# A two-layer hybrid decoder on one core: the first layer's feed-forward starts by token tile

## The chip, the core and the metric

The kernel runs on one core of a Trainium2 chip. Its time is device microseconds of one execution. In the texts below PE is TensorE, which multiplies matrices, DVE is VectorE, ACT is ScalarE, POOL is GpSimd, and SP is the queue from which the transfers are issued. PSUM is the memory into which PE writes, in banks of 128 x 512 floats; SBUF holds all other tiles.

## What is computed

256 tokens of width 2048 go through two layers. Each layer has a mixer (sliding-window attention beside an RWKV-7 recurrence) and a feed-forward network of width 5632. Both are framed by a modulation from a condition vector and by a layer norm. Cut to what matters here:

```python
mod = einsum('bd,de->be', silu(c), w_ada[l]) + b_ada[l]      # six vectors of 2048
sh_m, sc_m, gt_m, sh_f, sc_f, gt_f = split(mod)
u = x * (1 + sc_m) + sh_m
mix = concat([attention(u @ w_in[l]), rwkv7(u @ w_in[l])]) @ w_out[l]
x = layer_norm(alpha * x + gt_m * mix, ln1_w[l], ln1_b[l])
u = x * (1 + sc_f) + sh_f
gate, up = split(u @ w_gate_up[l])
x = layer_norm(alpha * x + gt_f * ((silu(gate) * up) @ w_down[l]), ln2_w[l], ln2_b[l])
```

## The kernel before, in words

**Tiles.** The 256 tokens are two token tiles of 128. The width of 2048 is 16 row blocks of 128 (`kts`, `kt`), over which every projection sums. A float32 product is made of three products of a faster format: each operand is split into a high part (its cast to that format) and a low part (what the cast lost), and PE adds high x high, high x low and low x high. For weights ACT makes the high part (line 380) and DVE the low part (line 381). For activations the two parts are the halves of a tile `u`, one for each row block.

**Weights.** `steps` (line 364) loads 512 KB at a time into one of four `raw` tiles and splits it, usually into three `hi` and two `lo` tiles. If it is given a `room`, it splits into tiles from there instead, so that the parts can be kept. `stream` (line 390) issues the products of a list of row blocks. For each token tile in `ts` and each 512 columns it issues lines 402 (high x high), 403 (the weights' low part) and 405 (the activations' low part). It returns the split weights, and a later call that is given them as `held` uses them again.

**The feed-forward's start.** `channel` (line 1115) ends the mixer: the last 512 columns of the output projection are finished for token tile 0 first and then for tile 1, since `SPLIT_O` is (8, 8). Behind each tile come the gate (line 1163), the residual (1164) and the statistics (1165), all on DVE. `normalise` then takes the mean and variance (1064), adds the epsilon (1066), raises to the power -1/2 on POOL (1067), and scales the tile's four pieces, two on DVE (1078) and two on ACT (1076).

`inputs` (line 1080) makes the `u` tiles out of the normalised rows `z`, eight row blocks at a time. It has two ways, chosen by `apart`. With `apart` 0 it calls `make_u`: PE transposes a pair of row blocks for both token tiles (354), ACT makes a float32 copy and the high part, 256 columns each (358, 360), and DVE subtracts (361). With `apart` 8 the first eight row blocks go by token tile:

```python
for t in range(2):
    for k4 in range(0, apart, 4):
        ... # four transposes of tile t (line 1100)
        V.tensor_scalar(uf, pt_[:, i * P:(i + 1) * P], a[:, kt:kt + 1], b[:, kt:kt + 1], ALU.mult, ALU.add)
        S.copy(u[:, 0, :], uf)
        V.tensor_tensor(u[:, 1, :], uf, u[:, 0, :].bitcast(F32), ALU.subtract)
    yield kts[0:apart], (t,)
```

These are lines 1105 (DVE), 1106 (ACT) and 1107 (DVE), with 128 columns each. The text calls what they make of one row block and one token tile a half. The products of tile 0 come with `room_ht2` (line 1131), which takes two `ht` tiles of 128 x 1024 for a row block's weights; the products of tile 1 reuse them. The pool has twelve `ht` tiles. Row blocks 8 to 15 always go through `make_u`, for both tiles at once.

The first block of 512 columns of gate and up, f = 0, is the one that runs while `inputs` yields (line 1206). Behind it stands the SiLU (1218). Blocks f = 1 to 10 use the finished `u` tiles. While f = 1 and later blocks run, and during f = 0 too, DVE also multiplies the rows by the norm's weight and adds its bias (1181, 1182; eight of each), which only the later residual needs.

**Work from elsewhere on DVE.** The modulation of what comes later is computed in between: `ada_steps` (line 246) loads 512 KB of `w_ada` into one of two `ast` tiles and adds it, scaled, to `aacc` on DVE (line 257; the first of a unit is line 255), sixteen times for a unit. Then PE transposes (277) and ACT sums (281). `pump` (line 331) moves it on behind every weight step. Its last units are needed by the second layer.

**The order.** A scheduler places every instruction, by priority and by its own estimate, when the program is built. Each engine then takes its instructions in that order. So a change in one place can move instructions on all engines.

Of the kernel before, what the change touches and what calls it, by code (L numbers as in the profile page):

```python
# [58 lines left out]
AB = (1, 1, 1, 1)  # L59
XB = 2  # L60
SPLIT_O = (8, 8)
SPLIT_F = (0, 8)
SPLIT_D = (1, 1)
TWO_PI = 2.0 * math.pi

# [2 lines left out]
def hybrid_trunk_kernel(  # L68
# [1046 lines left out]
    def channel(l, ys, wa, fp):  # L1115
# [52 lines left out]
        us = []  # L1168
        parts = inputs(fp, z, l, "ln1_w", "ln1_b", l, 4, 3, us, SPLIT_F[l])

# [181 lines left out]
```

## Time and profile before

| what | value |
|---|---|
| runs | 2698.06 us median of 3, 2688.91 to 2700.31 |
| profiled execution | 2694.28 us, of which 2692.6 are its span |
| mean granted clock of TensorE | 0.965 |
| PE busy | 2501.1 us |
| DVE busy | 1841.0 us |
| ACT busy | 1188.3 us |
| read from HBM | 622.08 MB |

The profile was taken on one execution, and times in it count from the span's start. The first layer's feed-forward begins near 636 us and the second layer's near 1935 us. An instruction's length in the profile overlaps a little with the next one's on the same engine, so the distance from start to start is the smaller number.

### The profile page before, as it was taken

The numbers are of one execution on the slowest core, as the hardware profiler recorded it, in microseconds if no ns is written. First come the engines' busy times: TensorE is split into PE (matmuls) and PEld (weight loads), VectorE is DVE, ScalarE is ACT, GpSimd is POOL, SyncE is SP. The second block draws the span as 40 slices with busy tenths as digits, with TensorE's granted clock in tenths as the row PEclk, the third lists the DMA queues.
The fourth block names the chain that finished last, engine by engine and source line by source line (L and its number), as shares of the span: only waits on it lengthen the run. The fifth ranks groups of instructions, "written<-read, shape, count | busy, mean of one in ns | idle before, by whom it ended". The sixth has DMA issues, their size and how long they took to land.

```text
span 2692.6 us, 41752 instructions
## 1 busy us (share of the span) xinstructions
PE 2501.1 (93%) x15325; PEld 2093.1 (78%) x15325; DVE 1841.0 (68%) x2469; ACT 1188.3 (44%) x2029; POOL 135.0 (5%) x355
## 2 busy tenths in 40 slices
PE   3788998788999999999999999979899999999997
PEld 2687886567888888888889877867688888888887
DVE  6866767979877777777788677555764545545456
ACT  2364452435444444444445544534444444344442
POOL 1002112000000000000000022110000000000000
PEclk9789998899999999999999999989999999999999
DMA  9968668688998888889878586424756656666654
GB/s 315 381 188 253 198 191 238 180 317 296 353 330 309 297 303 312 293 295 308 308 263 304 174 259 188 117 72 144 253 172 188 190 186 196 195 189 189 193 188 149
DMA packets 351999, 637.49 MB, mean 237 GB/s; under 512 B 75894, under 2 KB 142898, under 8 KB 350258
## 3 DMA queue, kind: packets, MB, share of 16 engines
q1 hardware_dynamic: 351794, 634.82, 71.6%
q8 instruction: 120, 1.97, 0.3%
q14 instruction: 85, 0.70, 0.1%
HBM read 622.08 MB, written 12.62 MB: 236 GB/s over the span
## 4 chain that ended last, share of the span: by engine, by line
PE 68%; DMA 8%; DVE 6%; ACT 2%; issue 1%; POOL 1%; SPq 0%; DVEq 0%; POOLq 0%; ACTq 0%
PE acc L403 19%; PE acc L402 19%; PE acc L405 19%; DMA ast<-in_w_ada_dram 3%; DVE aacc L257 2%; PE acc L414 2%; PE acc L415 2%; PE acc L416 2%; DVE lo L381 1%; DMA raw<-in_w_gate_up_dram 1%; PE mb L1225 1%; DMA raw<-in_w_out_dram 1%; DMA yf<-yd 1%; PE mb L277 1%; ACT pr L947 0%
## 5 line engine op out<-in xcount | busy, mean ns | idle before, releaser
L380 ACT CAST hi<-raw 128x1024 fp32r<-128x1024 f32 (+2 forms) x728 | 758.5, 1044 | 1110.8 <-PE acc L405 833.1
L381 DVE TENSOR_TENSOR lo<-raw,hi 128x1024 fp32r<-128x1024 f32 (+2 forms) x728 | 880.2, 1212 | 519.8 <-PE acc L403 347.1
L403 PE MATMUL acc<-lo,u 128*128 128x512 f32 x1568 | 513.4, 395 | 11.9 <-DVE lo L381 11.8
L405 PE MATMUL acc<-hi,u 128*128 128x512 f32 x1568 | 505.8, 391 | 0.0
L257 DVE SCALAR_TENSOR_TENSOR aacc<-ast,cond,aacc 128x1024 f32<-128x1024 f32 x300 | 384.1, 1280 | 127.8 <-DMA ast<-in_w_ada_dram 126.6
L402 PE MATMUL acc<-hi,u 128*128 128x512 f32 x1568 | 457.2, 393 | 0.9 <-ACT u L360 0.5
L403 PEld LDWEIGHTS acc<-lo,u 128*128 128x128 f32 x1568 | 293.8, 189 | 76.4 <-DVE lo L381 16.2
L402 PEld LDWEIGHTS acc<-hi,u 128*128 128x128 f32 x1568 | 294.9, 188 | 63.4 <-ACT sg L1218 0.9
L405 PEld LDWEIGHTS acc<-hi,u 128*128 128x128 f32 x1568 | 295.2, 188 | 61.8 <-issue 0.5
L403 PE MATMUL acc<-lo,ht 128*128 128x512 f32 (+1 forms) x720 | 243.6, 377 | 3.0 <-DVE lo L381 2.9
L405 PE MATMUL acc<-hi,ht 128*128 128x512 f32 (+1 forms) x720 | 242.2, 375 | 0.0
L414 PE MATMUL acc<-u,hi 128*128 128x256 f32 x720 | 206.1, 293 | 14.0 <-ACT hi L380 14.0
L402 PE MATMUL acc<-hi,ht 128*128 128x512 f32 (+1 forms) x720 | 217.0, 376 | 0.0
L415 PE MATMUL acc<-u,hi 128*128 128x256 f32 x720 | 204.5, 291 | 0.0
L416 PE MATMUL acc<-u,lo 128*128 128x256 f32 x720 | 193.1, 294 | 7.1 <-DVE lo L381 7.1
L403 PEld LDWEIGHTS acc<-lo,ht 128*128 128x128 f32 x720 | 135.0, 188 | 29.3 <-DVE lo L381 5.6
L414 PEld LDWEIGHTS acc<-u,hi 128*128 128x128 f32 x720 | 141.9, 197 | 19.3 <-ACT hi L380 14.9
L405 PEld LDWEIGHTS acc<-hi,ht 128*128 128x128 f32 x720 | 135.6, 188 | 24.2
L402 PEld LDWEIGHTS acc<-hi,ht 128*128 128x128 f32 x720 | 134.8, 188 | 24.4
L415 PEld LDWEIGHTS acc<-u,hi 128*128 128x128 f32 x720 | 141.7, 197 | 2.6 <-issue 1.6
L416 PEld LDWEIGHTS acc<-u,lo 128*128 128x128 f32 x720 | 133.8, 197 | 11.6 <-DVE lo L381 9.0
L1067 POOL TENSOR_TENSOR brs<-brs,mhalf 128x1 f32<-128x1 f32 x8 | 7.6, 955 | 1698.7 <-DVE brs L1066 772.1
(349 smaller groups left out, 2901.1 us busy)
## 6 DMA issues: line engine op xcount, KB each, us to landing
ast<-in_w_ada_dram SPq DMA_DIRECT2D x368, 512.0 KB
raw<-in_w_gate_up_dram SPq DMA_DIRECT2D x704, 256.0 KB
raw<-in_w_down_dram SPq DMA_DIRECT2D x176, 512.0 KB
raw<-in_w_in_dram SPq DMA_DIRECT2D x82, 512.0 KB
raw<-in_w_out_dram SPq DMA_DIRECT2D x64, 512.0 KB
raw<-in_w_in_dram SPq DMA_DIRECT2D x120, 256.0 KB
ast<-in_w_ada_dram SPq DMA_DIRECT2D x32, 256.0 KB
lnw<-in_ln_w_dram SPq DMA_DIRECT2D x4, 1024.0 KB
```

The costliest lines, as they stand in the source:

```text
L257: ins = V.scalar_tensor_tensor(acc, t, cond[:, j:j + 1], acc, ALU.mult, ALU.add)
L277: PE.transpose(b[:, i * P:(i + 1) * P], blocks[q + i], ident)
L380: S.copy(h, fl)
L381: ins = V.tensor_tensor(r, fl, h.bitcast(F32), ALU.subtract)
L402: PE.matmul(bt, lhsT=xh, rhs=hi[:, c0:c0 + w], start=st, stop=False)
L403: PE.matmul(bt, lhsT=xh, rhs=lo[:, c0:c0 + w], start=False, stop=False)
L405: PE.matmul(banks[t][q][:, 0:w], lhsT=xl, rhs=hi[:, c0:c0 + w], start=False, stop=sp_)
L414: PE.matmul(bt, lhsT=hi[:, c0:c0 + w], rhs=xh, start=st and opens, stop=False)
L415: PE.matmul(bt, lhsT=hi[:, c0:c0 + w], rhs=xl, start=False, stop=False)
L416: PE.matmul(bt, lhsT=lo[:, c0:c0 + w], rhs=xh, start=False, stop=sp_ and closes)
L1067: G.tensor_tensor(rs[:, 0:1], rs[:, 0:1], mhalf[:, 0:1], ALU.pow)
L1225: PE.transpose(b[:, i * T + t * P:i * T + (t + 1) * P], hh[t][:, (2 * k2 + i) * P:(2 * k2 + i + 1) * P], ident)
```

## The change

One number changes:

```diff
-SPLIT_F = (0, 8)
+SPLIT_F = (8, 8)
```

`channel` hands `SPLIT_F[l]` to `inputs` as `apart`. In the first layer row blocks 0 to 7 of block f = 0 now go by token tile: tile 0's transposes, halves and products, then tile 1's with the held weights. Eight times two ACTIVATEs of 256 columns and one subtraction (lines 358, 360, 361) become sixteen of lines 1105, 1106 and 1107. The products and the transposes are the same in number, and so is what is loaded. The order agrees with that of before up to the output projection's end, and again from the fourth block of the feed-forward to the last part of the second layer's mixer.

On DVE, around the statistics and the normalisation of both tiles (L1165 statistics, L1164 residual, L1064 mean and variance, L1066 epsilon, L1072 the bias of the scaling, L1078 scaling), this stood before:

```order
L1165 BN_STATS bst<-z 128x6
L1164 SCALAR_TENSOR_TENSOR z<-xres,z 128x512
L1064 BN_AGGR bmv<-bst 128x2
L1165 BN_STATS bst<-z 128x6
L1066 TENSOR_SCALAR brs<-bmv 128x1
L257 SCALAR_TENSOR_TENSOR aacc<-ast,cond,aacc 128x1024
L1064 BN_AGGR bmv<-bst 128x2
L1072 SCALAR_TENSOR_TENSOR brs<-bmv,brs 128x1
L1066 TENSOR_SCALAR brs<-bmv 128x1
L1078 TENSOR_SCALAR z<-z,brs 128x512 x2
```

And this stands there now (`ht<-raw,ht` is the low part of held weights, `aacc<-ast` the modulation):

```order
L381 TENSOR_TENSOR ht<-raw,ht 128x1024
L1165 BN_STATS bst<-z 128x6
L381 TENSOR_TENSOR ht<-raw,ht 128x1024
L1164 SCALAR_TENSOR_TENSOR z<-xres,z 128x512
L257 SCALAR_TENSOR_TENSOR aacc<-ast,cond,aacc 128x1024
L1064 BN_AGGR bmv<-bst 128x2
L381 TENSOR_TENSOR ht<-raw,ht 128x1024
L1165 BN_STATS bst<-z 128x6
L257 SCALAR_TENSOR_TENSOR aacc<-ast,cond,aacc 128x1024
L1066 TENSOR_SCALAR brs<-bmv 128x1
L1064 BN_AGGR bmv<-bst 128x2
L1066 TENSOR_SCALAR brs<-bmv 128x1
```

Three low parts of weights stand between these rows, a fourth stands just ahead of them behind the first residual, and two rows of the modulation stand ahead of the first epsilon where one stood behind it. Behind the scaling come one more low part and one more row of the modulation, and only then the first L1105.

Where the halves are made, DVE had one subtraction of 256 columns for each row block:

```order
L257 SCALAR_TENSOR_TENSOR aacc<-ast,cond,aacc 128x1024
L1181 TENSOR_TENSOR z<-z,lnw 128x512 x2
L361 TENSOR_TENSOR u<-uf,u 128x256
L257 SCALAR_TENSOR_TENSOR aacc<-ast,cond,aacc 128x1024
L1182 TENSOR_TENSOR z<-z,lnb 128x512 x2
L361 TENSOR_TENSOR u<-uf,u 128x256 x2
L257 SCALAR_TENSOR_TENSOR aacc<-ast,cond,aacc 128x1024
L381 TENSOR_TENSOR lo<-raw,hi 128x1024
```

Now it has, for row blocks 2 to 5 of tile 0:

```order
L257 SCALAR_TENSOR_TENSOR aacc<-ast,cond,aacc 128x1024
L1105 TENSOR_SCALAR uf<-mb,aco,bco 128x128 x2
L257 SCALAR_TENSOR_TENSOR aacc<-ast,cond,aacc 128x1024
L1107 TENSOR_TENSOR u<-uf,u 128x128 x2
L1105 TENSOR_SCALAR uf<-mb,aco,bco 128x128
L1181 TENSOR_TENSOR z<-z,lnw 128x512
L1105 TENSOR_SCALAR uf<-mb,aco,bco 128x128
L257 SCALAR_TENSOR_TENSOR aacc<-ast,cond,aacc 128x1024
L1107 TENSOR_TENSOR u<-uf,u 128x128
L1182 TENSOR_TENSOR z<-z,lnb 128x512
L1107 TENSOR_TENSOR u<-uf,u 128x128
```

A row of the modulation stands between nearly every L1105 and its L1107, and between that and the next L1105.

In the second layer's mixer, near its end, DVE had rows of a recurrence's close (L851, L852, L854: its norm) among the rows of the rotary embedding (L894 to L899):

```order
L894 TENSOR_TENSOR ra<-qk,cosk 128x640
L895 TENSOR_TENSOR rb<-qk,sink__147 128x640
L851 TENSOR_REDUCE vr<-sq 128x8
L852 TENSOR_SCALAR vr<-vr 128x8
L898 TENSOR_TENSOR qr<-ra,rb 128x5x32
L899 TENSOR_TENSOR qr<-ra,rb 128x5x32
L898 TENSOR_TENSOR qr<-ra,rb 128x5x32
L899 TENSOR_TENSOR qr<-ra,rb 128x5x32
```

Now the rows of the embedding follow one another and the first scores (L932) come next:

```order
L898 TENSOR_TENSOR qr<-ra,rb 128x5x32
L899 TENSOR_TENSOR qr<-ra,rb 128x5x32
L898 TENSOR_TENSOR qr<-ra,rb 128x5x32
L899 TENSOR_TENSOR qr<-ra,rb 128x5x32
L894 TENSOR_TENSOR ra<-qk,cosk 128x640
L895 TENSOR_TENSOR rb<-qk,sink__147 128x640
L932 ISA pr,mx<-acc,wmask 128x256
```

The first of the close's rows stands behind eight of the scores now, and a row of the inversion (L752), which stood behind four of them, behind ten.

## The prediction

> **What bounds the kernel now.** I read the page's first part, then the stretches, then the idle tables and single instructions of the first layer's feed-forward start. The page says that TensorE is the busy engine, and the stretches say where it isn't.
>
> ```profile
> PE 2501.1 (93%) x15325; PEld 2093.1 (78%) x15325; DVE 1841.0 (68%) x2469; ACT 1188.3 (44%) x2029; POOL 135.0 (5%) x355
> ```
>
> Columns of a stretch: its length, then busy time and count of PE, weight loads, DVE, ACT and POOL, granted clock, DMA share, GB/s.
>
> ```profile
> 636.00:700.00 64.00, 55.32 (x246) 44.03 (x247) 57.70 (x81) 38.55 (x69) 2.45 (x2) 0.92 0.85 294
> 700.00:1000.00 300.00, 299.59 (x1359) 247.20 (x1358) 230.47 (x218) 136.04 (x198) 0.00 (x0) 1.00 0.91 315
> 1700.00:1870.00 170.00, 152.54 (x1429) 122.22 (x1428) 100.31 (x257) 76.33 (x192) 15.14 (x37) 0.91 0.32 94
> 1935.00:1995.00 60.00, 53.79 (x238) 43.72 (x237) 43.16 (x83) 31.40 (x53) 1.92 (x2) 0.91 0.54 185
> ```
>
> Row 1 is the stage that the change edits. PE has 8.7 us idle there, but DVE has only 6.3 us free in 64: both engines are short. Row 2 is what follows: PE has 0.4 us idle in 300, so a microsecond lost in row 1 is never won back there, nor one gained taken away. Row 4 is the second layer's same stage, whose form the first is to take: there DVE has 16.8 us free in 60. What fills DVE in row 1 and not in row 4 is the modulation of the layers to come (grouped view of 636 to 700; busy time, mean ns):
>
> ```profile
> L257 DVE SCALAR_TENSOR_TENSOR aacc<-ast,cond,aacc 128x1024 f32<-128x1024 f32 x15 | 19.2, 1282 | 0.2 <-DMA ast<-in_w_ada_dram 0.2
> ```
>
> The hole in row 1, by single instructions (start, length):
>
> ```profile
> 635.38 0.39 PE L405 MATMUL acc<-ht,yl 128*128 128x512 f32 x1
> 634.72 0.68 DVE L1163 TENSOR_TENSOR z<-acc,gtb 128x512 f32<-128x512 f32 x1
> 636.12 0.68 DVE L1163 TENSOR_TENSOR z<-acc,gtb 128x512 f32<-128x512 f32 x1
> 636.72 0.68 DVE L1165 BATCH_NORM_STATS2 bst<-z 128x6 f32<-128x512 f32 x1
> 638.64 0.14 DVE L1066 TENSOR_SCALAR brs<-bmv 128x1 f32<-128x1 f32 x1
> 638.85 1.52 POOL L1067 TENSOR_TENSOR brs<-brs,mhalf 128x1 f32<-128x1 f32 x1 [108.69 <-DMA ast<-in_w_ada_dram]
> 640.40 0.16 DVE L1072 SCALAR_TENSOR_TENSOR brs<-bmv,brs 128x1 f32<-128x1 f32 x1 [0.27 <-POOL brs L1067]
> 642.95 0.99 DVE L1078 TENSOR_SCALAR z<-z,brs 128x512 f32<-128x512 f32 x2
> 643.86 1.28 DVE L257 SCALAR_TENSOR_TENSOR aacc<-ast,cond,aacc 128x1024 f32<-128x1024 f32 x1
> 645.56 0.80 PE L402 MATMUL acc<-hi,u 128*128 128x512 f32 x1 [0.47 <-ACT u L360]
> 695.73 0.62 PE L405 MATMUL acc<-hi,u 128*128 128x512 f32 x2
> ```
>
> The output projection ends at 635.8; the first product of the feed-forward starts at 645.56, 9.8 us later, and block f=0 ends at 696.2 (695.73 and two products). Between lies a chain on DVE: gate and residual, statistics, the power on POOL, normalisation. DVE issues it in program order with no idle beside 0.27 us, so what is put among these rows delays them in full.
>
> **The change part by part.** Prices are distances from one start to the next on a busy engine. These rows give L381 1.14, L361 0.33, L257 1.20 (653.58 less 652.38); above, L1163 and its kin 0.60, the pair L1078 0.91.
>
> ```profile
> 650.91 1.22 DVE L381 TENSOR_TENSOR lo<-raw,hi 128x1024 fp32r<-128x1024 f32 x1
> 652.05 0.42 DVE L361 TENSOR_TENSOR u<-uf,u 128x256 fp32r<-128x256 f32 x1
> 652.38 1.28 DVE L257 SCALAR_TENSOR_TENSOR aacc<-ast,cond,aacc 128x1024 f32<-128x1024 f32 x1
> 653.58 0.42 DVE L361 TENSOR_TENSOR u<-uf,u 128x256 fp32r<-128x256 f32 x1
> ```
>
> The new instructions run in the second layer: two L1105 take 0.64, two L1107 0.40, one L1182 0.60, an ACT cast 0.3.
>
> ```profile
> 1954.76 0.72 DVE L1105 TENSOR_SCALAR uf<-mb,aco,bco 128x128 f32<-128x128 f32 x2
> 1955.40 0.68 DVE L1181 TENSOR_TENSOR z<-z,lnw 128x512 f32<-128x512 f32 x1
> 1956.00 0.48 DVE L1107 TENSOR_TENSOR u<-uf,u 128x128 fp32r<-128x128 f32 x2
> 1956.40 0.68 DVE L1182 TENSOR_TENSOR z<-z,lnb 128x512 f32<-128x512 f32 x1
> 1957.00 0.72 DVE L1105 TENSOR_SCALAR uf<-mb,aco,bco 128x128 f32<-128x128 f32 x2
> L1106 ACT CAST u<-uf 128x128 fp32r<-128x128 f32 x16 | 4.5, 296 | 5.0 <-DVE uf L1105 4.8
> ```
>
> *Work.* DVE gains 16 L1105 (5.1 us) and 16 L1107 (3.2) and loses 8 L361 (2.6): +5.7 us. PE has the same products and transposes; ACT swaps 16 ACTIVATEs of 256 columns (L358, L360) for 16 casts and gains time. By amount alone DVE's 6.3 free microseconds would hide the 5.7: the low end is 0.
>
> *First term, the start.* The order of DVE decides. After the product with the gate at 634.72 (all rows before it stand as before) come, up to the first L1105: six rows of gate, residual and statistics 3.6; five L381 5.7 (four of them weights pulled ahead into `ht`); three L257 3.6 (the first two of their loads are issued where they are now); eight small rows 0.8; the wait for POOL's power, 1.76 from 638.64 to 640.40, with 0.3 of rows under it, 1.5; the pair L1078 0.9; the L1105 itself 0.3. That is 16.4: 651.1. With ACT's 0.3 the first product starts at 651.4, 5.9 us later than 645.56.
>
> *Second term, the pass by tiles.* Until the last low half of rows 0 to 7 DVE has 15 L1105 (4.8), 16 L1107 (3.2), eight affine rows L1181/L1182 (4.8), the second tile's pair L1078 (0.9), three L381 (3.4) and eleven L257 (13.2): 30.3 us. Each L257 needs its `ast` tile; there are two of them, and one takes 3.98 to reload:
>
> ```profile
> 634.83 3.98 DMA ast<-in_w_ada_dram
> 711.81 0.91 PE acc L402 x4
> 663.68 0.44 PE mb L354 x4
> ```
>
> So one tile goes round in 3.98 + 1.28 = 5.26, one L257 per 2.6 us, where the order leaves 2.4: some 1.6 us of waits (0 to 4). The last low half is out at 651.1 + 30.3 + 1.6 = 683.0. PE needs only 16 x 6 x 0.228 = 21.9 us for these halves and waits between them for L1107. The 12 `ht` tiles hold six row blocks at two each, so blocks 6 and 7 of the first tile stand behind blocks 0 and 1 of the second, and their L381 among those three.
>
> *Third term, the rest.* When the low half of block 4 of tile 1 is out, 1.2 us before 683.0, PE has 20 products and four transposes to go, 5.0 us: 686.8. Then eight row blocks of 12 products (21.9), two groups of transposes (0.9) and eight of the modulation (0.9): 710.5, against 696.2. That is +14.3, rounded to +14; with the first term alone +6, with longer waits for `ast` +17. The second layer's `SPLIT_F` is as before, and the program's order agrees again from the fourth block on, up to the second layer's mixer tail (below), which I take at 0 (-2 to +2).
>
> The profiled execution took 2694.28 us (span 2692.6): 2694.28 + 14 = 2708. It lies 3.8 under the median of the runs, 2698.06; on that, 2712.
>
> **The clock.** Idle PE is granted half its clock, and keeps it for some microseconds:
>
> ```profile
> 638.00:640.00 2.00, 0.00 (x0) 0.00 (x0) 2.00 (x5) 0.00 (x0) 1.15 (x1) 0.57 0.32 131
> 646.00:648.00 2.00, 2.00 (x6) 1.52 (x6) 2.00 (x4) 1.43 (x3) 0.00 (x0) 0.50 0.79 229
> 648.00:650.00 2.00, 2.00 (x12) 1.65 (x11) 2.00 (x5) 0.50 (x2) 0.00 (x0) 0.87 0.58 135
> 646.78 0.43 PE acc L402
> ```
>
> Products at half clock take 0.43. In the new pass PE waits about 3 us for the first L1107 and about 5 us between the tiles; while DVE is the bound, slow products hide in those waits, so the sum has nothing for them. The Trainium skill, "TensorE: Matmul & The Clock Gate", section "Part 1: The HAM clock gate", says that a window of about 3.4 us without work halves the clock and that a busy window restores it. By that, the 5 us wait would halve it once more, 1.7 us on top (an estimate from the page's window): 2714. The rows agree in kind: 0.57 within 4 us of the last product, 0.87 about 4 us after the first.
>
> **The rivals.**
>
> *The clock stays at half through the pass.* For it: the pass is cut by waits. Then PE is the bound: 651.4 + 96 x 0.43 + 1.8 for 16 transposes = 694.5, and 23.7 more make 718.2: +22, 2720. Against it: once PE is the bound it no longer waits, and the clock comes back.
>
> *The tail of the second layer's mixer pays it back.* There the order of DVE changes too: the rope and score rows move ahead of a close's L851 and L854. PE waited there:
>
> ```profile
> PE acc L906 <- DVE qr L899: 6.0, 1, 6.0
> PE acc L925 <- DVE mx L932: 5.1, 1, 5.1
> ```
>
> If both go, 11.1 us come back: 2712 - 11 = 2701, not slower. Against it: an L752 of the inversion moves behind score rows at the same place, so the likely balance is near 0. It decides if the first of those two waits ends over 5 us sooner.
>
> *It works as in the second layer.* There the first product comes 8.1 us after the projection (9.8 here):
>
> ```profile
> 1934.85 0.39 PE L405 MATMUL acc<-ht,yl 128*128 128x512 f32 x1
> 1943.22 0.80 PE L402 MATMUL acc<-ht,u 128*128 128x512 f32 x1 [2.74 <-ACT u L1106]
> ```
>
> 1.6 us sooner, and the small waits behind it gone: about -2, 2696. For it: the same program text, and PE waits nowhere behind 1943.22 in that block. Against it: the grouped view of that stretch has no L257 at all, where the first layer's has fifteen; it needs the first L1105 before 645.
>
> **How the numbers follow.** The sum's case gets 0.60 (+9 to +19), the slow clock 0.13, the tail 0.14, the second layer's way 0.13. A measurement here tells 0.5%, 13.5 us. Just over half of the first case and all of the second lie above: slower 0.48. The rest of the first and most of the last two lie within: same 0.48. A gain over 13.5 us needs the last two at once: faster 0.04. The range 2699 to 2720 takes in the tail's 2701 and the slow clock's 2720 and leaves out the 2696.
>
> **What would show it.** First step: the first product on `ht` 15 to 16 us after the projection's last, with four L381 128x1024 between the two L1163 and the L1078 of the first tile. Second: PE waiting for L1107 several times in the pass, about 10 us in all, and no DVE idle beside waits for `ast`. Third: the first L1218 some 14 us later. A first product within 11 us, or no PE waits on L1107, would prove the sum wrong; so would a tail shorter by over 5 us.

## The result and the profile after

The changed kernel takes 2710.69 us, median of 7 runs (2701.90 to 2714.87), beside 2693.95 us of the kernel before (7 runs). The ratio is 1.0055, 95% interval 1.0040 to 1.0070: slower by 10.8 to 18.9 us. The forecast was +14, a range of 2699 to 2720. The profiled execution took 2703.67 us, 9.4 more than the one of before.

The page's first part for after, and then three stretches, which answer to rows 1, 2 and 4 shown of before. The first is longer, since the stage is.

```profile
PE 2499.9 (93%) x15325; PEld 2089.5 (77%) x15325; DVE 1846.2 (68%) x2493; ACT 1186.0 (44%) x2029; POOL 133.3 (5%) x355
```

```profile
632.00:709.00 77.00, 56.13 (x233) 43.48 (x234) 65.08 (x106) 33.70 (x68) 1.06 (x2) 0.84 0.75 247
709.00:1000.00 291.00, 288.50 (x1305) 237.07 (x1304) 215.21 (x202) 130.91 (x192) 0.00 (x0) 1.00 0.88 307
1945.00:2005.00 60.00, 53.57 (x240) 43.19 (x239) 43.08 (x83) 31.29 (x53) 1.94 (x2) 0.94 0.55 188
```

DVE gained 5.2 us over the whole program (the sum had 5.7), and TensorE's work is the same. In the edited stage TensorE is idle for 20.9 of 77 us, where it was for 8.7 of 64. Behind it (second row) it has 2.5 us free in 291, so nothing is won back there, and the second layer's same stage (third row) is as it was.

The start, by single instructions (start, length, engine). Between the second L1163 and the first scaling L1078 stand three L381 into `ht`, and two L257 with them; a fourth L381 stood ahead of that L1163 at 631.21.

```profile
631.20 0.39 PE L405 MATMUL acc<-ht,yl 128*128 128x512 f32 x1
633.02 0.68 DVE L1163 TENSOR_TENSOR z<-acc,gtb 128x512 f32<-128x512 f32 x1
633.62 1.22 DVE L381 TENSOR_TENSOR ht<-raw,ht 128x1024 fp32r<-128x1024 f32 x1
635.36 1.21 DVE L381 TENSOR_TENSOR ht<-raw,ht 128x1024 fp32r<-128x1024 f32 x1
637.09 1.28 DVE L257 SCALAR_TENSOR_TENSOR aacc<-ast,cond,aacc 128x1024 f32<-128x1024 f32 x1
638.46 1.16 DVE L381 TENSOR_TENSOR ht<-raw,ht 128x1024 fp32r<-128x1024 f32 x1
640.13 1.27 DVE L257 SCALAR_TENSOR_TENSOR aacc<-ast,cond,aacc 128x1024 f32<-128x1024 f32 x1
641.32 0.15 DVE L1066 TENSOR_SCALAR brs<-bmv 128x1 f32<-128x1 f32 x1
642.12 0.16 DVE L1072 SCALAR_TENSOR_TENSOR brs<-bmv,brs 128x1 f32<-128x1 f32 x1 [0.30 <-POOL brs L1067]
642.32 1.01 DVE L1078 TENSOR_SCALAR z<-z,brs 128x512 f32<-128x512 f32 x2
645.65 0.72 DVE L1105 TENSOR_SCALAR uf<-mb,aco,bco 128x128 f32<-128x128 f32 x2
645.88 1.51 ACT L1076 ACTIVATE z<-z,brs 128x512 f32<-128x512 f32 x2
647.63 0.79 PE L402 MATMUL acc<-ht,u 128*128 128x512 f32 x1 [2.67 <-ACT u L1106]
```

The output projection ends at 631.59 in this execution (635.77 in before's), so times are best counted from there. The first product comes 16.0 us later, where it came 9.8 later: +6.2. From the epsilon to POOL's power took 0.80 here (641.32 to 642.12), where the sum takes 1.76 from before, so the first L1105 came 1.0 sooner than summed. ACT gave it back: the first cast L1106 stood behind the second tile's L1076, and the first product started 1.4 later behind that L1105 than summed.

The pass. Two of DVE's five waits for `ast`, the last low half, and the last products of f = 0:

```profile
655.52 1.28 DVE L257 SCALAR_TENSOR_TENSOR aacc<-ast,cond,aacc 128x1024 f32<-128x1024 f32 x1 [1.26 <-DMA ast<-in_w_ada_dram]
678.66 1.28 DVE L257 SCALAR_TENSOR_TENSOR aacc<-ast,cond,aacc 128x1024 f32<-128x1024 f32 x1 [1.49 <-DMA ast<-in_w_ada_dram]
681.04 0.61 DVE L1107 TENSOR_TENSOR u<-uf,u 128x128 fp32r<-128x128 f32 x2
708.74 0.61 PE L405 MATMUL acc<-hi,u 128*128 128x512 f32 x2
```

TensorE's waits in the stage (us in total, times, longest):

```profile
PE mb L1100 <- DVE z L1078: 11.4, 1, 11.4
PE acc L402 <- ACT u L1106: 5.7, 2, 3.1
PE acc L405 <- DVE u L1107: 3.1, 3, 1.4
PE mb L1100 <- DVE uf L1105: 1.0, 1, 1.0
```

The first row is the start. The others are TensorE's waits for halves, 9.8 us, of which 2.67 still belong to the start. DVE never idles in the pass but for `ast` (1.26, 0.42, 0.78, 0.42 and 1.49, 4.4 us in all). Block f = 0 ends at 709.20 (708.74 and two products), 77.6 us after the projection, where it took 60.4: the stage is **17.2 us longer**. The first L1218 comes 15.2 later (77.4 behind the projection for 62.2), where the prediction had some 14. The whole is longer by less, so something came back elsewhere. It is at the end of the second layer's mixer. The first L906 of that layer and the output projection's last product on `yl`, in before and then in after:

```profile
1774.28 0.48 PE L906 MATMUL acc<-ident,qr 128*128 128x128 f32 x1 [5.95 <-DVE qr L899]
1923.96 0.40 PE L405 MATMUL acc<-hi,yl 128*128 128x512 f32 x1
```

```profile
1790.25 1.16 PE L906 MATMUL acc<-ident,qr 128*128 128x128 f32 x3 [5.83 <-DVE qr L899]
1934.09 0.39 PE L405 MATMUL acc<-hi,yl 128*128 128x512 f32 x1
```

That stretch took 149.7 us before and 143.8 after: 5.9 less. In after's waits there the one for the rope, which ends where the stretch begins (5.8, in before 6.0), is still there, and the 5.1 for the scores' `mx` (L925), shown of before, is gone:

```profile
PE acc L906 <- DVE qr L899: 7.1, 2, 5.8
PE m L749 <- DVE den L949: 2.6, 1, 2.6
```

17.2 less 5.9 is 11.3. That the two profiled executions differ by 9.4 comes from places where the order is the same or nearly so: the projection's end came 4.2 sooner, from f = 0 to the first L906 it took 2.9 longer (1081.0 against 1078.1), and 0.7 less behind the tail. Run 5 shows below that such differences are chance.

### The profile page after: what moved, and what is told of

It is laid out like the page before. It is cut to its first block, busy times and chain, and to the rows that moved or that the text cites. A ratio compares the mean times of both kernels' runs of the same rounds, so it can differ in the third digit from the quotient of the medians.

```text
span 2702.0 us, 41760 instructions
## 1 busy us (share of the span) xinstructions
PE 2499.9 (93%) x15325; PEld 2089.5 (77%) x15325; DVE 1846.2 (68%) x2493; ACT 1186.0 (44%) x2029; POOL 133.3 (5%) x355
## 4 chain that ended last, share of the span: by engine, by line
PE 68%; DMA 8%; DVE 7%; ACT 1%; issue 1%; SPq 0%; POOL 0%; DVEq 0%; ACTq 0%; POOLq 0%
PE acc L403 19%; PE acc L405 19%; PE acc L402 19%; DMA ast<-in_w_ada_dram 5%; DVE aacc L257 2%; DVE lo L381 2%; PE acc L416 2%; PE acc L415 2%; PE acc L414 2%; DMA yf<-yd 1%; PE mb L1225 1%; DMA raw<-in_w_gate_up_dram 1%; PE mb L277 1%; DMA qkv<-stg 0%; DMA raw<-in_w_out_dram 0%
## 5 line engine op out<-in xcount | busy, mean ns | idle before, releaser
L380 ACT CAST hi<-raw 128x1024 fp32r<-128x1024 f32 (+1 forms) x720 | 749.9, 1044 | 1111.5 <-PE acc L405 829.4
L381 DVE TENSOR_TENSOR lo<-raw,hi 128x1024 fp32r<-128x1024 f32 (+1 forms) x720 | 870.4, 1212 | 513.1 <-PE acc L403 355.3
L403 PE MATMUL acc<-lo,u 128*128 128x512 f32 x1536 | 504.1, 395 | 12.6 <-DVE lo L381 12.6
L405 PE MATMUL acc<-hi,u 128*128 128x512 f32 x1536 | 497.8, 392 | 0.0
L257 DVE SCALAR_TENSOR_TENSOR aacc<-ast,cond,aacc 128x1024 f32<-128x1024 f32 x300 | 384.4, 1281 | 136.4 <-DMA ast<-in_w_ada_dram 134.9
L402 PE MATMUL acc<-hi,u 128*128 128x512 f32 x1536 | 449.7, 393 | 0.0
L403 PEld LDWEIGHTS acc<-lo,u 128*128 128x128 f32 x1536 | 288.2, 189 | 77.6 <-DVE lo L381 18.4
L405 PEld LDWEIGHTS acc<-hi,u 128*128 128x128 f32 x1536 | 289.9, 189 | 60.9 <-issue 0.5
L402 PEld LDWEIGHTS acc<-hi,u 128*128 128x128 f32 x1536 | 289.2, 189 | 60.1 <-issue 0.3
```

Of the source, the lines that this page charges most:

```text
L257: ins = V.scalar_tensor_tensor(acc, t, cond[:, j:j + 1], acc, ALU.mult, ALU.add)
L380: S.copy(h, fl)
L381: ins = V.tensor_tensor(r, fl, h.bitcast(F32), ALU.subtract)
L402: PE.matmul(bt, lhsT=xh, rhs=hi[:, c0:c0 + w], start=st, stop=False)
L403: PE.matmul(bt, lhsT=xh, rhs=lo[:, c0:c0 + w], start=False, stop=False)
L405: PE.matmul(banks[t][q][:, 0:w], lhsT=xl, rhs=hi[:, c0:c0 + w], start=False, stop=sp_)
```

## The experiments

Ten kernels were run, each in five rounds beside the kernel before. Theory 1 is the prediction's: DVE's order holds the start and then the pass, up to the last low half. The rivals are told in the texts on record. Those count the stage up to the first L1218 (62.2 before, 77.4 after); on TensorE, f = 0 ends 60.4 and 77.6 us after the projection.

All in one table; the times in us are worked out from single instructions. "Gap": projection's last product to the feed-forward's first. "Last half": to the start of the last L1107 (a row of the profile can hold two of them; the second counts). "f = 0": to its last product's end, and to the first L1218. "Between": from there to the second layer's first L906. "Tail": from that L906 to the last product on `yl`.

| kernel | ratio to before, 95% | gap | last half | f = 0 (L1218) | between | tail |
|---|---|---|---|---|---|---|
| before | | 9.8 | | 60.4 (62.2) | 1078.1 | 149.7 |
| after | 1.0055 (1.0040 to 1.0070) | 16.0 | 49.8 | 77.6 (77.4) | 1081.0 | 143.8 |
| 1 room only | 1.0005 (0.9991 to 1.0018) | 16.7 | | 69.2 (69.1) | 1082.0 | 141.2 |
| 2 after, held | 1.0060 (1.0041 to 1.0079) | 9.9 | 50.5 | 75.5 (75.3) | 1074.3 | 149.9 |
| 3 after, quiet | 1.0044 (1.0031 to 1.0057) | 15.6 | 34.7 | 67.4 (67.2) | 1082.7 | 142.8 |
| 4 held and quiet | 1.0051 (1.0033 to 1.0069) | 9.9 | 35.9 | 65.9 (66.5) | 1084.2 | 151.0 |
| 5 before, L851 moved | 1.0009 (0.9996 to 1.0022) | 9.8 | | 60.5 (62.4) | 1081.1 | 150.4 |
| 6 before, quiet | 1.0018 (1.0005 to 1.0030) | 9.8 | | 57.4 (57.2) | 1089.9 | 148.0 |
| 7 four row blocks | 1.0005 (0.9991 to 1.0018) | 14.8 | 29.6 | 67.5 (67.9) | 1076.9 | 147.5 |
| 8 held, quiet, affine late | 1.0025 (1.0012 to 1.0037) | 9.9 | 33.7 | 64.1 (64.8) | 1087.0 | 145.5 |
| 9 before, other pace | 1.0006 (0.9994 to 1.0019) | 9.8 | | 60.5 (62.2) | 1093.5 | 143.0 |
| 10 before, held | 0.9976 (0.9962 to 0.9989) | 9.2 | | 60.9 (60.4) | 1079.2 | 143.0 |

How far chance goes is seen in it too. Before, 5 and 9 have the same order in the stage, and it took 60.4, 60.5 and 60.5. The stretch "between" isn't as steady: 1078.1 and 1081.1 in before and 5, with the same order up to its end.

**Run 1: the first term alone.** Before, with `ht` tiles for the weights of the first eight row blocks.

```diff
-                                      ts, room_ht2 if ts == (0,) else None, held if ts == (1,) else None)
+                                      ts, room_ht2 if ts == (0,) or (l == 0 and kts[0] == 0) else None, held if ts == (1,) else None)
```

> The first row blocks go through make_u for both tiles, as before, but the first eight blocks' weights are split into ht tiles, as after: the low parts are pulled ahead, and nothing else of the change is there. The stage from the output projection's last product to the first L1218 took 62.2 us before and 77.4 after, the gap to the feed-forward's first product 9.8 and 16.0. Theory 1 (DVE's order: rows put among gate, statistics and scaling delay the start one for one): four or five L381 of 1.14 and one more L257 of 1.20 ahead of the second tile's scaling, so a gap of 15 to 17 and a stage of 67 to 70; the whole +5 to +8. Rival 2 (the halves' greater amount of DVE work is the cost, where the low parts stand is not): gap 10 to 11, stage 62 to 64, the whole within 2 of before.

Measured: gap 16.7, f = 0 at 69.2. Both lie in theory 1's range; rival 2's 10 to 11 and 62 to 64 are out.

```profile
633.77 0.39 PE L405 MATMUL acc<-ht,yl 128*128 128x512 f32 x1
650.87 0.80 PE L402 MATMUL acc<-ht,u 128*128 128x512 f32 x1 [0.47 <-ACT u L360]
```

With no half made in the new way, the room for the weights alone lets the low parts run ahead of the normalisation and costs 8.8 us of stage. The whole didn't show it: it came out between 2.4 less and 4.8 more than before, where the text had expected +5 to +8. The parts give +8.8 in the stage, +3.9 between and -8.5 in the tail, +4.2. This tail can't be compared in full, since 26 of TensorE's records that stand behind the first L906 in the other kernels stand ahead of it here.

**Run 2: the start put right.** After, with the low parts of row blocks 2 to 7 behind the first scaling. `gate` holds the name of the last L1078 while tile 0's weights are split:

```diff
-            anchor[:] = [ins.ins.name]
+            anchor[:] = [ins.ins.name]; [tc.add_manual_dep(ins.ins, g, order, reason="behind the scaling") for g in gate if i0 >= 2]
...
+                        gate[:] = scaled[0] if l == 0 and ts == (0,) else []; held = stream(gu, 1024, kts, us[kts[0]:], ...
```

> After, with the low parts of row blocks 2 to 7 held behind the first tile's scaling. The same rows stand on DVE up to the last low half, in another order. Theory 1 (DVE is the bound up to the last low half): the first product some 11 us after the projection (16.0 after), but the four low parts come back in the pass, the last L1107 stays 48 to 50 us after the projection and the stage 75 to 78. Rival 3 (the late start is the cost, the pass follows on PE): the stage gets the 4.6 us back, 72 to 73.

Measured: the first product comes 6.1 us sooner than in after (9.9 against 16.0), the last half doesn't (50.5 against 49.8; 48 to 50 expected), and f = 0 ends only 2.1 sooner. Theory 1's stage (75 to 78) fits, and rival 3's 72 to 73 doesn't. What TensorE no longer waits for at the start it waits for in the pass:

```profile
PE acc L402 <- ACT u L1106: 8.9, 4, 3.8
PE mb L1100 <- DVE z L1078: 5.5, 1, 5.5
PE acc L405 <- DVE u L1107: 4.2, 4, 3.3
```

So the first term isn't a cost of its own in after. DVE's rows up to the last half are one queue, and a row taken from its head comes back in it.

**Run 3: the modulation out of the pass.** Its steps start again behind f = 0, at a higher pace; nothing is left out.

```diff
-AF_ = (0.75, 0.55)
+AF_ = (0.82, 0.55)
...
-                    held = None
+                    held, pace[0] = None, pace[0] * l
```

> After, with no step of the modulation started while f = 0 of the first layer runs (made up later at a higher pace; nothing is left out). Theory 1: the start is as late as after (16), but the pass loses nine L257 (10.8) and their waits for ast (4.4), so the last L1107 comes 35 to 40 us after the projection (50.0 after), PE becomes the bound, and the stage takes 68 to 71; the whole +6 to +9 against before. Rival 4 (TensorE at half clock bounds the pass): the stage stays at 75 to 77. Rival 2 (the halves' own 8 us of DVE work is the cost): likewise over 73.

Measured: five L257 in the stage for seventeen, the last half at 34.7 (35 to 40 expected), the first L1218 at 67.2 (68 to 71 expected), f = 0 at 67.4. The last half came 15.1 sooner, and TensorE was the bound from there on, so f = 0 got 10.2 of it. Rival 4, the clock, falls with it. The clock was at half here too, into the third stretch of four microseconds, and the last half came all the same:

```profile
652.00:656.00 4.00, 1.78 (x4) 1.17 (x4) 4.00 (x8) 3.41 (x6) 0.00 (x0) 0.50 0.73 237
656.00:660.00 4.00, 2.20 (x6) 1.52 (x6) 4.00 (x8) 0.20 (x1) 0.00 (x0) 0.50 0.63 180
660.00:664.00 4.00, 4.00 (x19) 3.28 (x18) 3.85 (x13) 1.60 (x6) 0.00 (x0) 0.88 0.28 110
```

Rival 2 falls as well: the halves' own rows are all still there. The whole, +8.4 to +15.4, is more than the +6 to +9 expected. The parts give +7.0 in the stage, +4.6 between and -6.9 in the tail, +4.7; the other 4 to 11 us aren't seen in the profiled execution and stay open.

**Run 4: both edits.**

> Low parts held behind the scaling and no modulation during f = 0 together. Theory 1: gap about 11, last L1107 some 35 us after the projection, stage 62 to 66, the whole within 4 of before. If the start and the pass aren't both DVE's order, the stage stays over 70.

Measured: gap 9.9, last half 35.9, first L1218 at 66.5, just over the range. The start and the pass are DVE's order, as theory 1 has it. The whole was 8.9 to 18.6 over before, not within 4. The tail came out as in before (151.0), and the stretch between took 6.1 more. The modulation put off isn't free later.

**Run 5: one row of the tail.** Before, with the third close's L851 behind the rope's last L899. The text takes this for DVE's whole order of after; the trace shows below that it isn't.

```diff
-            V.reduce_sum(vr, sq.rearrange("p (e s) -> p e s", s=CH), axis=AX.X)
+            ins = V.reduce_sum(vr, sq.rearrange("p (e s) -> p e s", s=CH), axis=AX.X); l and g == 2 and tc.add_manual_dep(ins.ins, rots[-1], order, reason="behind the rope")
```

> Before, with one edit at the end of the second layer's mixer: the third close's L851 is held behind the rope's L899, so that DVE's rows there stand as in after; the first layer is untouched. From the last product of the attention (L981) to the output projection's last product on yl (L405, hi) the profiles read 81.3 us in before and 76.8 in after, 77.1 in run 1 and 77.1 in run 3 (order as in after), 81.5 in run 2 and 81.4 in run 4 (order as in before). Theory 5 (the tail's order pays back 4.5): 76.5 to 77.5 there, the whole 3 to 6 us under before. Rival 6 (chance of the executions): 81, the whole as before. It is also a second look at before's first layer: the blocks f = 1 to 5, last product to last product, took 224.8 in before and 227.7 to 230.2 in the five others; about 225 here if the change costs them 4 to 5 us, 228 to 230 if before's profile was lucky.

Measured: from L981 to `yl` 81.9, tail 150.4, the whole as before. The wait that after lost is still here, 4.9 us on L925. L851's place alone gains nothing. Theory 5, that DVE's order in the tail pays back, isn't tested by it, because the edit moved that one row. TensorE's products for the first scores and DVE's first row on them stand like this in before and in after; the last line is DVE's row in this run:

```profile
1781.43 1.13 PE L925 MATMUL acc<-qT 64*128 64x256 f32 x8
1787.94 0.42 DVE L932 CUSTOM_DVE_ANT_0 pr<-acc,wmask 128x256 f32<-128x256 f32 x1
```

```profile
1796.82 1.95 PE L925 MATMUL acc<-qT 64*128 64x256 f32 x8
1799.10 0.42 DVE L932 CUSTOM_DVE_ANT_0 pr<-acc,wmask 128x256 f32<-128x256 f32 x1
```

```profile
1789.34 0.42 DVE L932 CUSTOM_DVE_ANT_0 pr<-acc,wmask 128x256 f32<-128x256 f32 x1
```

Counted from the first L906, the products end equally soon: 8.3, 8.5 and 8.3 us behind it. DVE takes them at 13.7, 8.9 and 13.5. In before and in run 5 it first issues the rest of the third group of the rope, rows of the close and the L894 and L895 of the fourth group. So the wait that after lost is one for DVE's order, and run 5 left it as it was.

TensorE's order differs as well, and most of the time is gained there. Its last products of the attention (L981) and the last transposes of the close (L858), in before and then in after:

```profile
1842.67 0.48 PE L981 MATMUL acc<-pts,vt 128*64 128x128 f32 x3
1859.09 0.60 PE L858 MATMUL oc<-ident,sq 128*128 128x128 f32 x4
```

```profile
1851.88 0.60 PE L858 MATMUL oc<-ident,sq 128*128 128x128 f32 x4
1857.46 0.48 PE L981 MATMUL acc<-pts,vt 128*64 128x128 f32 x3
```

From this L981 to the last product on `yl` before takes 81.3 and after 76.6, which is 4.7 of the 5.9. Behind it before has 34 more of TensorE's records, of the recurrence (L811 to L825) and its close (L845, L846, L858). In after they stand ahead of the L981, which comes 1.2 sooner even so. The two differences go together in all twelve kernels. In after and runs 1, 3 and 7 to 10 the first L932 starts 8.9 to 11.1 us behind the first L906, the 34 stand ahead, and the stretch from L981 takes 76.6 to 77.6. In before and runs 2, 4, 5 and 6 it starts at 13.5 to 15.5, they stand behind, and the stretch takes 81.3 to 82.9. That the 34 fill the time of the lost wait fits this, but no run separates the two.

The text also asks about blocks f = 1 to 5. Counted alike from the end of f = 0, they took 228.9 here and 227.0 in before (the text has 224.8), so before's profiled execution was a little lucky there.

**Run 6: before without the modulation in f = 0.** The edit of run 3, with `SPLIT_F` as in before.

> Before (make_u for all row blocks), with no step of the modulation started while f = 0 of the first layer runs, made up later at the higher pace. Theory 1: PE isn't held by DVE in before's stage beyond the 9.8 us of the start, so the stage comes down by 0 to 2 (60 to 62.2); the later blocks f = 1 to 5 carry the modulation and take 228 to 230 as in run 3. The whole +1 to +6. Rival 7 (the modulation costs wherever the first layer's start is, and is free later): stage 58, the whole -4.

Measured: f = 0 at 57.4, 3.0 less, and the first L1218 at 57.2, where rival 7 had 58 and theory 1, which missed here, had 60 to 62.2. So DVE's load holds before's stage too, a little. The whole was slower all the same, by 1.3 to 8.1: the stretch between took 11.8 more.

**Run 7: half the dose.** `SPLIT_F = (4, 8)`.

> After with four row blocks by tile in the first layer instead of eight: half the halves, and two low parts fewer pulled ahead of the scaling into ht, but two into lo in their place. Theory 1: start 14 to 16 us after the projection, a pass with half the rows by tile and 4 to 6 us fewer waits, stage 69 to 73 (62.2 with none, 77.4 with eight). The tail's order is nearly as after, so 4 come back; the whole +4 to +10. Rival 2 (the halves' amount of work alone): half of 15, but with the start at 10 to 12.

Measured: gap 14.8, first L1218 at 67.9, just under the 69 to 73. Of the 17.2 us, four row blocks bring 7.1. The tail gives 2.2 back, and the whole isn't told from before (2.4 less to 4.8 more), where +4 to +10 was expected.

**Run 8: the affine rows out of the pass as well.** Run 4, and in the first layer L1181 behind the last L1107:

```diff
-                    V.tensor_mul(zq, zq, lw[:, o:o + 512])
+                    ins = V.tensor_mul(zq, zq, lw[:, o:o + 512]); l or tc.add_manual_dep(ins.ins, last[0], order, reason="behind the halves")
```

> After with the low parts held behind the scaling, no modulation during f = 0, and the affine rows L1181 and L1182 held behind the last halves, in the first layer. Theory 1: gap 9.9, last L1107 32 to 35 us after the projection (35.6 in run 4), stage 63 to 66; the tail stands as in after, 77 (81.4 in run 4). The whole within 4 of before. If the affine rows matter in the pass by their 4.8 us, the stage is 62; if not, 66 as in run 4.

Measured: last half 33.7 (35.9 in run 4), first L1218 at 64.8, tail 145.5. The whole was 3.2 to 10.0 over before, not within 4. The affine rows' 4.8 us bring about 2, since DVE isn't the bound all the time any more: it is idle for 4.9 us up to the last half. Even with everything else out of its way, the pass by tiles ends f = 0 3.7 us later than before's pass did, and 6.7 later than run 6, which also has no modulation in it.

**Run 9: the tail's order, with the first layer as in before.** `AF_ = (0.76, 0.55)`, nothing else.

> Before, with the modulation's pace in the first layer at 0.76 in place of 0.75. DVE's rows at the feed-forward's start stand as in before; one unit's steps come a little earlier later on, and with that the order at the end of the second layer's mixer comes out as in run 7, on TensorE too (there the tail took 77.6, in after 76.6, in before 81.3). Theory 5b (TensorE's order in the tail, which run 5 left alone, pays 4 to 5 us): tail 77 to 78, stage 61.3, the whole 2 to 6 us under before. Rival 6 (it belongs to the first layer's change, or to chance): tail 81 to 82, the whole as before. Third look at before's blocks f = 1 to 5: 224 to 227.

Measured: f = 0 at 60.5, tail 143.0 (from L981 to `yl` 77.0). The short tail comes with its order and without any change in the first layer's start. Theory 5b names TensorE's order alone, but DVE's and ACT's are nearly those of run 7 here too, so its time is met and its cause isn't separated. The whole doesn't follow: between, where a good part of the order is new, the profiled execution took 15.4 more, and the whole, 1.6 less to 5.1 more than before where 2 to 6 less was expected, leaves open how much of that is the new pace and how much is chance.

**Run 10: a version that beats both.** Before, with the low parts of row blocks 1 to 7 behind the second tile's scaling: run 2's edit with `i0 >= 1` and `scaled[1]`. The tail comes out nearly as in after on TensorE, DVE and ACT.

> Before, with the low parts of row blocks 1 to 7 of f = 0 held behind the second tile's scaling in the first layer. One L257 that stood between the rows of statistics goes behind the first scaling with them, no row is added, and the tail's order comes out as in after on TensorE and ACT. Theory 1 (what stands among the statistics and the scaling delays the start): gap 8.5 to 9.5 in place of 9.8, stage 60 to 62, since the rows up to the last L361 are the same; with theory 5b the tail 76.6 to 77.5 and the whole 3 to 7 us under before. If the start's order doesn't count, the gap stays 9.8.

Measured: the whole is 3.0 to 10.2 us faster than before, which no other kernel here is. Its tail:

```profile
1775.66 1.16 PE L906 MATMUL acc<-ident,qr 128*128 128x128 f32 x3 [5.11 <-DVE qr L899]
1918.62 0.39 PE L405 MATMUL acc<-hi,yl 128*128 128x512 f32 x1
```

The gap is 0.6 shorter, yet f = 0 ends no sooner on TensorE (60.9). The tail is 6.7 shorter, and with +0.5 in the stage and +1.1 between that makes -5.1, inside the measured interval. So in the profiled execution, what was meant for the start paid at the tail, through the scheduler. That the tail makes the whole faster rests on this sum: run 9 has the same tail and isn't faster.

## Why the prediction was right, and where its terms were off

**What bounds.** Right: DVE in its order sets the start and the pass. Runs 2 and 3 show it from both sides: moving rows within the queue leaves the last half where it was, and taking rows out of it moves the last half up by what they took: ten L257 fewer up to there (12.0) and the 4.4 of waits are 16.4, of which 15.1 were measured, since DVE then waits once for TensorE's transposes (1.0).

**First term, the start.** Right: +5.9 forecast, +6.2 measured. Within it, POOL's power was sized 1.0 too long, and ACT's L1076 ahead of the first cast, 1.4, was left out. The two nearly cancel, which is luck.

**Second term, the pass.** The mechanism was right and the size was off. The last low half was to be out 47.2 us after the projection (683.0 less 635.8). It was out at 50.0, 2.8 later. The term that was mis-sized is "some 1.6 us of waits (0 to 4)" for `ast`: they were 4.4. It priced a load at the 3.98 of one, and the loads that end the waits took longer. The chain that ended last has 4.59, 4.15, 4.41 and 4.74 in after's pass, of which the first and the last are:

```profile
650.85 4.59 DMA ast<-in_w_ada_dram
673.83 4.74 DMA ast<-in_w_ada_dram
```

That makes some 2 of the 2.8 us, an estimate from these lengths and the waits behind them. That an average of one L257 per 2.4 us hides how unevenly the rows come may be the rest, which isn't shown. TensorE's waits for halves were about as long as forecast (9.8 for "about 10") but lay mostly at ACT's cast L1106 (5.7) rather than at L1107 (3.1).

**Third term, the rest.** Right: 27.5 forecast, 27.6 measured. With the 2.8 of the pass the stage came to +17.2, where the sum had +14.3.

**The tail "I take at 0".** Wrong by 5.9 in the good direction. By the prediction's own sign, "a tail shorter by over 5 us", the sum is proved wrong in this term. The rival that it pays back had 11.1 as price if both waits go; one of the two went, not the one that was to decide it. The step that failed is the balance with the L752 of the inversion: in after's waits it shows with 0.4 us (L756 for `yx` L752). In its place the first scores came 4.8 sooner on DVE, and TensorE had the end of the recurrence done ahead of the attention's last products. Which of the two orders brings the time stays open.

**The sum.** +17.2 and -5.9 make +11.3, in the measured 10.8 to 18.9, beside the forecast's +14. The two misses, +2.9 and -5.9, went against each other; that the middle of the measurement lies so close to the forecast is in part luck.

**The clock at half.** It did stay longer than the prediction's reading of before: to 656.9, 9 us after the first product, and again after the 3.1 us wait between the tiles.

```profile
646.00:650.00 4.00, 2.07 (x4) 1.16 (x4) 4.00 (x8) 2.83 (x5) 0.00 (x0) 0.50 0.73 247
650.00:654.00 4.00, 2.93 (x7) 2.35 (x8) 4.00 (x8) 0.02 (x1) 0.00 (x0) 0.50 0.79 235
654.00:658.00 4.00, 4.00 (x15) 2.96 (x14) 2.74 (x6) 0.87 (x3) 0.00 (x0) 0.63 0.59 173
```

As forecast, it cost little: DVE was busy in these rows but for its 1.26 us wait for `ast` in the third, and the last half followed DVE's rows. The rival's +22 didn't come.

**The second layer's way.** Wrong as a guide for the first layer, and given 0.13 beforehand. The second layer's stage has no L257; after has three of them and five L381 on DVE ahead of the first L1105, and its first product came at 16.0 and not at 8.0 (the prediction's rows give 8.0, not 8.1).

## What to carry to other kernels

When an engine issues in order and is nearly full, cost a reordering by what stands in its queue up to the last thing that another engine needs: moving a row forward or back in it gains little (2.1 of 17.2 us in run 2), taking it out moves that last thing up by nearly its length (15.1 for 16.4 us in run 3). Room for more buffers is not free: it lets the producer run ahead, here by five 1.14 us rows into the one chain that the next stage waits for. When a scheduler places the instructions, compare the whole program's order on every engine, and price what moved far from the edit: here a third of the stage's loss was won back 1100 us further on. Before a run is read as a test of an order, look in its trace whether that order is there.

## What the runs showed that was not expected

Executions differ by chance more than the effect of this change (before's took 2686.6 to 2703.8 us in 35 runs), but not everywhere. Up to the output projection nearly the same order stands in all twelve kernels, and it ended between 631.6 and 639.1 us. The stage, counted from a local start, repeats to about 0.1 us with the same order (60.4, 60.5, 60.5), and the tail of 150 us to about one (149.7 and 150.4; with before's order on TensorE in runs 2 and 4, 149.9 and 151.0). So such a stretch can decide between two mechanisms where a total can't. It has a limit: runs 7 and 9 have nearly the same order in the tail and took 147.5 and 143.0. Most of that lies between 30 us behind the first L906 and the last L981, with the granted clock at 0.87 and at 1.00:

```profile
1808.38:1848.48 40.10, 38.13 (x360) 27.89 (x360) 22.82 (x88) 19.05 (x63) 1.93 (x2) 0.87 0.02 6
1819.00:1855.16 36.16, 33.19 (x358) 24.45 (x358) 22.41 (x87) 18.85 (x63) 1.64 (x1) 1.00 0.02 6
```

In these kernels TensorE's clock came back some time after its last longer stop, and not a fixed time after the first product: 0.87 within four microseconds in before, but 9 us in after, where the products stopped for 1.36 us ahead of 651.07 and then ran on. In the twelve kernels it was back 2.2 to 5.9 us behind the last stop of 0.4 us or more, but 2.2 to 9.3 us behind the first product. The row at which they stop, and the clock after the later wait:

```profile
651.07 1.22 PE L405 MATMUL acc<-ht,u 128*128 128x512 f32 x2 [1.36 <-DVE u L1107]
```

```profile
668.00:670.00 2.00, 1.55 (x5) 0.84 (x4) 1.58 (x5) 1.05 (x1) 0.00 (x0) 0.50 0.50 98
```

The Trainium skill, "TensorE: Matmul & The Clock Gate", section "Part 1: The HAM clock gate", speaks of a busy window of about 3.4 us that restores it, and says that the window runs freely and doesn't start with the work. From 651.07 to 656.9 are 5.8 us without a wait, which have room for one such window, so the trace agrees. In runs 5 and 6 the clock was back after 2.2 us, less than the window, so by the page it holds the stop of 0.47 us ahead of the first product as well. The page gives an idle window of about 3.4 us for the halving. It did come a second time, with 0.50 from 668 to 670, after a wait of only 3.1 us with one of 1.0 us and four transposes ahead of it, so the measured wait is a little shorter than the page's window. As DVE was the bound, the 1.7 us that the prediction worked out from it can't be told in the time.
